# Input also laid out transposed; first chunk in four steps of input piece, weight piece and products; sum of squares from the pieces; identity products first

## Chip, core and metric

The kernel runs on one core of a Trainium2 chip. The metric is the time of one execution on the device in microseconds (us), as the median of several runs. Five engines work side by side and meet at semaphores: TensorE (PE: products and transposes into PSUM), VectorE (DVE), ScalarE (ACT), GpSimd (POOL) and SyncE (SP), which here only issues DMA transfers. An engine works through its own instructions in a fixed order.

## What is computed

Two macaron layers over 256 tokens of 1024 channels. The part in question is the start of the first feed-forward block (FFN):

```python
def rms_norm(x, gain):
    x32 = x.astype(jnp.float32)
    y = x32 * lax.rsqrt(jnp.mean(x32 * x32, axis=-1, keepdims=True) + EPS)
    return (y * gain.astype(jnp.float32)).astype(x.dtype)

def swiglu_ffn(x, w_in, w_out):
    gate, up = jnp.split(x @ w_in, 2, axis=-1)
    return (jax.nn.silu(gate) * up) @ w_out
...
for layer in range(DEPTH):
    g = norm_gains[layer]
    h = swiglu_ffn(rms_norm(x, g[0]), ffn_w_in[layer, 0], ffn_w_out[layer, 0])
    x = x + 0.5 * rms_norm(h, g[1])
    ...
```

After it come a causal convolution module or a gated linear recurrence, and a second FFN, in each layer.

## The kernel before

Tokens lie in two tiles of 128 (`xs[0]`, `xs[1]`, index t). An FFN has 11 chunks of 256 hidden channels. For each chunk, SP brings four weight pieces of 128x1024 fp32 for the way up (`w1`) and two for the way down (`w2`), each 512 KB, from one long array (`weight`, L115). A landed piece lies in one of 4 buffers `raw`; ACT rounds it to fp32r (`wh`) and DVE takes the rest (`wl = raw - wh`, `split`, L130 to L132). A piece's transfer waits until DVE has read the piece four before it. Every product is three PE products, hi by hi, hi by lo and lo by hi (`mm3`, L134 to L137).

The input needs to stand with channels on partitions. `pre_norm` (L160) does that: PE transposes 128x128 blocks through PSUM (L168), ACT multiplies by the gain and rounds (L172, into `xth`), DVE takes the rest (L178, into `xtl`). The factor 1/rms of a token is not needed for the products: `mean_square` (L151) sums the squares on ACT with an accumulator (L156), POOL adds and takes the power -0.5 (L146, L148, L158), and the factor goes into the sigmoid's scale and the products' finish (`up`, L316 to L320). Chunk 0 has the tokens on PSUM partitions (`project_both`, L222: 48 products of 512 columns, half for each token tile). All later chunks (`channels`, L274) have hidden channels there, 48 products of 256 columns for each half b of a chunk (L281 to L283), and need the token factors as a row tile, which `token_scales` (L262, L268) makes with two fp32 products.

At the start SP issues the first half of tile 0 of the input (256 KB), the gains, the second half, tile 1 (512 KB) and then the weight pieces in the order of the array: w1 of chunk 0, w2 of chunk 0, w1 of chunk 1, and so on. The Tile scheduler sets the order of each engine's instructions; `tc.issue_after` holds an instruction back behind another. The body calls `ffn(0, 0, first_weights, constants)`; `constants(c)` is called after chunk c and makes tables for later stages. `xs` is read again in `post_norm` (L200), at the end of the FFN.

Of the kernel before, what the change touches and what calls it, by code (L numbers as in the profile page):

```python
# [8 lines left out]
F32 = mybir.dt.float32  # L9
# [7 lines left out]
P = 128  # L17
D = 1024
# [22 lines left out]
def trunk_kernel(  # L41
    ctx: ExitStack,
    tc: tile.TileContext,
    x_in: bass.AP,
    wts: bass.AP,
    cols: bass.AP,
    rows: bass.AP,
# [20 lines left out]
    def b4(dtype=F32):  # L68
        return new(sb, [P, 1024], dtype, "b4", 10)
# [34 lines left out]
    nc.sync.dma_start(xs[0][:, :512], x_in[0, :P, :512])  # L104
    nc.sync.dma_start(gcol, cols)
    nc.sync.dma_start(xs[0][:, 512:], x_in[0, :P, 512:])
    nc.sync.dma_start(xs[1], x_in[0, P:, :])

    stream = [0]
    ahead = []  # L110
    last_hi = [None]
    last_split = [None]
    last_raw = [None]

    def weight(fine=False):  # L115
        n, half = divmod(stream[0], 2)
        stream[0] += 1
        src = new(sb, [P, 1024], F32, "raw", 4)
        last_raw[0] = nc.sync.dma_start(src, wts[n, :, half * 1024 : half * 1024 + 1024]).ins
# [3 lines left out]
        with ExitStack() as held:  # L123
            if stream[0] <= 4:
                held.enter_context(tc.issue_after(last_hi[0]))
            for a in range(0, 1024, step):
                split(hi[:, a : a + step], lo[:, a : a + step], src[:, a : a + step])
        return hi, lo

    def split(dst_h, dst_l, src):  # L130
        last_split[0] = act.copy(dst_h, src).ins  # L131
# [19 lines left out]
    def mean_square(src):  # L151
        junk = b4()
        ss = tiny(2)
        for n in range(2):
            sl = slice(n * 512, (n + 1) * 512)
            act.activation(junk[:, sl], src[:, sl], AF.Square, accum_out=ss[:, n : n + 1])  # L156
        tot = tiny()
        pool.tensor_tensor(tot, ss[:, 0:1], ss[:, 1:2], op=ALU.add)  # L158
        return rsqrt(tot, 1.0 / D, EPS)

    def pre_norm(t, gi):
        src = xs[t]
        hi, lo = xth[:, t * D : (t + 1) * D], xtl[:, t * D : (t + 1) * D]
        for h in range(2):
            pt = tr()
            for j in range(4):
                k = h * 4 + j
                pe.transpose(pt[:, j * P : (j + 1) * P], src[:, k * P : (k + 1) * P], ident)  # L168
            for j in range(4):
                k = h * 4 + j  # L170
                g = gcol[:, gi * KD + k : gi * KD + k + 1]
                last_hi[0] = act.activation(hi[:, k * P : (k + 1) * P],  # L172
                                            pt[:, j * P : (j + 1) * P], AF.Copy, scale=g).ins
# [8 lines left out]
        if gi == 0:  # L182
            return hi, lo, None
        return hi, lo, mean_square(src)

    def transposed(src, hi, lo, n, base, gain=None):
        pt = tr()
# [10 lines left out]
    def post_norm(t, accs, gain, share, bias=None):  # L198
# [17 lines left out]
        for n in range(2):  # L216
# [5 lines left out]
    def project_both(xt, ws):  # L222
        o = [mm(), mm()]
        for t, i in ((0, 0), (0, 1), (1, 0), (1, 1), (0, 2), (0, 3), (1, 2), (1, 3)):
            hi, lo, _ = xt[t]
            wh, wl = ws[i]
            for k in (2 * i, 2 * i + 1):
                sl = slice((k % 2) * 512, (k % 2) * 512 + 512)
                kp = slice(k * P, (k + 1) * P)
                mm3(o[t], hi[:, kp], lo[:, kp], wh[:, sl], wl[:, sl], k == 0, k == KD - 1)  # L230
        return o

    def project(t, xt, ws):
        o = mm()
# [55 lines left out]
    def start(gi, before):  # L290
        first = pre_norm(0, gi)
        before()
        second = pre_norm(1, gi)
        if gi == 0:
            with tc.issue_after(last_split[0]):
                return [(*first[:2], mean_square(xs[0])), (*second[:2], mean_square(xs[1]))]
        return [first, second]

    def ffn(layer, which, before, extra=None):
        base = layer * 3 + (0 if which == 0 else 2)  # L300
        xt = start(base, before)
        accs = [None, None]
        w1, w2, hid, raw, both = {}, {}, {}, {}, {}

        def fetch(c):
            if c not in w1:
                fine = c == 0 or extra is not None and c == 1
                w1[c] = ahead.pop() if ahead else [weight(fine) for _ in range(4)]
                w2[c] = [weight(fine) for _ in range(2)]

        def up(t, c, o):
            if o is None:
                o = project(t, xt[t], w1[c])
            r = xt[t][2]
            sig = narrow("e")
            act.activation(sig, o[:, :CH], AF.Sigmoid, scale=r)  # L316
            g = narrow("e")
            dve.scalar_tensor_tensor(g, o[:, :CH], r, sig, op0=ALU.mult, op1=ALU.mult)
            h = narrow("e")
            dve.scalar_tensor_tensor(h, o[:, CH:], r, g, op0=ALU.mult, op1=ALU.mult)  # L320
            raw[t, c] = h

        def turn(t, c):
            hi, lo = narrow("hid", F32R), narrow("hid", F32R)
            transposed(raw.pop((t, c)), hi, lo, 2, 0)
            hid[t, c] = blocks(hi, lo, 2)

        def up_both(c, b):
            fetch(c)
            if b == 0:  # L330
                both[c] = b4(F32R)
            gu = channels(w1[c], (b * P, CH + b * P), scales)
            h = narrow("e")
            act.activation(h, gu[:, :SEQ], AF.Sigmoid)  # L334
            dve.tensor_tensor(h, h, gu[:, :SEQ], op=ALU.mult)  # L335
            dve.tensor_tensor(h, h, gu[:, SEQ:], op=ALU.mult)  # L336
            hi = both[c][:, b * SEQ : (b + 1) * SEQ]
            lo = both[c][:, 512 + b * SEQ : 512 + (b + 1) * SEQ]
            split(hi, lo, h)
            for t in range(NT):  # L340
                ts_ = slice(t * P, (t + 1) * P)
                hid.setdefault((t, c), []).append((hi[:, ts_], lo[:, ts_]))

        def down(t, c):
# [370 lines left out]

    made = {}

    def first_weights():
        ahead.append([weight(True) for _ in range(4)])

    def constants(c):
        if c == 2:
            made["steps"] = tap_spectrum()
        if c == 4:
            made["steps"].pop(0)()
        if 5 <= c < 9:
            made["steps"].pop(0)()
        if c == 9:
            with tc.issue_after(last_split[0]), tc.issue_after(last_raw[0]):
                made["lower"] = lower_bound()  # L730

    def store(t):
# [4 lines left out]
    rest = ffn(0, 0, first_weights, constants)  # L737
    rest = conv_mixer(0, made["spectrum"], rest)
    rest = ffn(0, 1, rest)
    rest = ffn(1, 0, rest)  # L740
# [102 lines left out]
```

## Time and profile before

| | |
|---|---|
| median of 3 runs | 1032.33 us (1032.0 to 1032.75) |
| the profiled execution's own time | 1030.74 us |
| its span, first to last instruction | 1029.0 us |
| PE busy | 1004.7 us (98%) |
| DVE, ACT, POOL busy | 705.6, 504.7, 71.0 us |
| mean granted clock of PE | 0.996 |
| DMA | 181.14 MB, mean 176 GB/s |

The profile is of one execution. Its span is 1.74 us shorter than the time of the same execution. Shares of busy time are a mean over stages; for this change the first 42 us count. A row of the timeline gives the start, the length from the first start to the last end, the engine, line and operation, and in brackets the idle time of the engine ahead of it with what ended it. PE's products overlap one another, so that the distance from start to start, and not the length, is what one of them costs in a row of them.

### The profile page before, as it was taken

Reading aid. Unit: us, or ns where it says so; the run is one execution under the profiler, and the core shown is the slowest. Engines: PE = TensorE matmul, PEld = TensorE weight load, DVE = VectorE, ACT = ScalarE, POOL = GpSimd, SP = SyncE. Lnnn points to the kernel's source line nnn. Section 1 sums busy time; section 2 is a strip of 40 time slices with the busy share of each in tenths; the row PEclk is TensorE's granted clock in tenths of the full one; section 3 lists DMA queues with packets and bytes.
Section 4 is the critical chain, followed back from the end, with each engine's and each line's share of the span. In section 5 each row is a group of like instructions: output and inputs, shape, how many; then the busy total and the mean of one; then the engine's idle time right before and its main releaser. Section 6 shows DMA issues by size and latency. Waiting matters only on the chain. (4 is left out here: it accounts for less than half of the span.)

```text
span 1029.0 us, 16850 instructions
## 1 busy us (share of the span) xinstructions
PE 1004.7 (98%) x6676; PEld 913.2 (89%) x6676; DVE 705.6 (69%) x1092; ACT 504.7 (49%) x852; POOL 71.0 (7%) x116
## 2 busy tenths in 40 slices
PE   7999999999899999999999999999999999999997
PEld 6999999888779999998899999989888879999996
DVE  6766666899887565658675656677676586666663
ACT  7544444764485444446544444574143473444441
POOL 1000000000010000000100000021343020000000
PEclk9999999999999999999999999999999999999999
DMA  7756464843536465647464646555222555564641
GB/s 254 259 198 212 156 211 142 270 164 111 182 101 226 168 199 170 223 152 241 144 206 163 205 164 226 185 202 179 87 84 91 176 175 186 161 215 155 215 143 41
DMA packets 50510, 181.14 MB, mean 176 GB/s; under 512 B 5985, under 2 KB 6113, under 8 KB 50432
## 3 DMA queue, kind: packets, MB, share of 16 engines
q1 hardware_dynamic: 50432, 180.07, 52.6%
q8 instruction: 52, 0.85, 0.3%
q14 instruction: 26, 0.21, 0.1%
HBM read 179.00 MB, written 1.05 MB: 175 GB/s over the span
## 5 line engine op out<-in xcount | busy, mean ns | idle before, releaser
L132 DVE TENSOR_TENSOR wl<-raw,wh 128x1024 fp32r<-128x1024 f32 (+1 forms) x386 | 400.6, 1059 | 200.4 <-ACT wh L131 196.8
L131 ACT CAST wh<-raw 128x1024 fp32r<-128x1024 f32 (+1 forms) x386 | 336.5, 923 | 275.4 <-PE mm L282 127.5
L281 PE MATMUL mm<-xth,wh 128*128 128x256 f32 x1408 | 396.3, 281 | 0.0
L282 PE MATMUL mm<-xtl,wh 128*128 128x256 f32 x1408 | 396.3, 281 | 0.0
L283 PE MATMUL mm<-xth,wl 128*128 128x256 f32 x1408 | 396.0, 281 | 0.0
L281 PEld LDWEIGHTS mm<-xth,wh 128*128 128x128 f32 x1408 | 265.8, 189 | 3.2 <-DVE e L335 0.7
L282 PEld LDWEIGHTS mm<-xtl,wh 128*128 128x128 f32 x1408 | 265.1, 188 | 2.6
L283 PEld LDWEIGHTS mm<-xth,wl 128*128 128x128 f32 x1408 | 266.1, 189 | 0.5 <-DVE wl L132 0.2
L136 PE MATMUL acc<-wl,b 128*128 128x512 f32 x352 | 137.8, 391 | 0.0
L137 PE MATMUL acc<-wh,b 128*128 128x512 f32 x352 | 137.7, 391 | 0.0
L135 PE MATMUL acc<-wh,b 128*128 128x512 f32 x352 | 137.6, 391 | 0.0
L137 PEld LDWEIGHTS acc<-wh,b 128*128 128x128 f32 x352 | 66.1, 188 | 14.1
L135 PEld LDWEIGHTS acc<-wh,b 128*128 128x128 f32 x352 | 66.1, 188 | 11.5
L136 PEld LDWEIGHTS acc<-wl,b 128*128 128x128 f32 x352 | 66.1, 188 | 11.4
L334 ACT ACTIVATE e<-ga 128x256 f32<-128x256 f32 x80 | 33.4, 418 | 79.8 <-DVE ga L286 79.8
L242 PE MATMUL mm<-wh,xth 128*128 128x512 f32 x176 | 70.7, 401 | 0.0
L243 PE MATMUL mm<-wl,xth 128*128 128x512 f32 x176 | 70.1, 398 | 0.0
L286 DVE TENSOR_TENSOR ga<-mm,scales 128x512 f32<-128x512 f32 x88 | 60.2, 685 | 12.4 <-PE mm L283 12.2
L146 POOL TENSOR_SCALAR tiny<-tiny 128x1 f32<-128x1 f32 (+1 forms) x30 | 8.4, 281 | 802.6 <-ACT b L212 711.5
L131 ACT CAST b<-e 128x256 fp32r<-128x256 f32 x80 | 32.4, 405 | 53.2 <-DVE e L336 53.2
L246 PE MATMUL mm<-wh,xtl 128*128 128x512 f32 x176 | 49.8, 397 | 0.0
L132 DVE TENSOR_TENSOR b<-e,b 128x256 fp32r<-128x256 f32 x80 | 33.8, 422 | 21.3 <-ACT b L131 21.3
(156 smaller groups left out, 877.4 us busy)
## 6 DMA issues: line engine op xcount, KB each, us to landing
raw<-wts SPq DMA_DIRECT2D x328, 512.0 KB, 5.0
b<-rows SPq DMA_DIRECT2D x10, 512.0 KB, 6.1
out_dram<-x SPq DMA_DIRECT2D x4, 256.0 KB, 2.1
x<-x_in SPq DMA_DIRECT2D x2, 256.0 KB, 2.8
x<-x_in SPq DMA_DIRECT2D x1, 512.0 KB, 4.2
b<-dft SPq DMA_DIRECT2D x1, 371.0 KB, 4.6
ca<-masks SPq DMA_DIRECT2D x1, 192.0 KB, 4.8
b<-w_dw SPq DMA_DIRECT2D x1, 124.0 KB
```

Of the source, the lines that this page charges most:

```text
L131: last_split[0] = act.copy(dst_h, src).ins
L132: dve.tensor_tensor(dst_l, src, dst_h.bitcast(F32), op=ALU.subtract)
L135: pe.matmul(o, lh, rh, start=first, stop=False)
L136: pe.matmul(o, lh, rl, start=False, stop=False)
L137: pe.matmul(o, ll, rh, start=False, stop=last)
L242: pe.matmul(o, hi[:, kp], wh[:, sl], start=k == 0, stop=False)
L243: pe.matmul(o, hi[:, kp], wl[:, sl], start=False, stop=False)
L246: pe.matmul(o, a, w, start=False, stop=h == 1 and n == 3)
L281: pe.matmul(og, wh[:, cs], xkh[:, k], start=k == 0, stop=False)
L282: pe.matmul(og, wh[:, cs], xkl[:, k], start=False, stop=False)
L283: pe.matmul(og, wl[:, cs], xkh[:, k], start=False, stop=k == KD - 1)
L286: dve.tensor_tensor(pair(res), pair(o), scales.unsqueeze(1).broadcast_to([P, 2, SEQ]), op=ALU.mult)
```

## The change

The host also lays the input out transposed, as `x_turned`: four pieces of 128 partitions by two channel blocks by 256 tokens (256 KB each). A new function `boot` makes chunk 0:

- 22 fp32 products of the 128x128 identity with itself, into a PSUM tile that nothing reads, stand first on PE.
- Then four steps follow, kept in this order on ACT, DVE, PE and SP by `behind`. Step i takes input piece i (ACT rounds its two blocks, DVE takes the rests, from SBUF and for both token tiles at once), weight piece i, the six products of token tile 0 and the six of token tile 1. There are no transposes by PE in it.
- The squares of each piece are made by ACT in SBUF without an accumulator, and added by DVE to a running sum. In step 3, between the products of the two token tiles, PE multiplies that sum by a column of ones (4 products of 128x1), DVE finishes the mean and POOL takes the power, for both token tiles in one instruction.
- The accumulators of chunk 0 come from the pool `acc`, not `mm`.
- w1 of chunk 1 is fetched before w2 of chunk 0, and all pieces of chunks 0 and 1 are split in halves of 512 columns (as before).
- The gains are loaded by a DMA that ACT issues. `xs` is loaded from `x_in` (two DMAs of 512 KB) after chunk 3.

```diff
+        warm = tr()
+        for j in range(22):
+            sl = slice(j % 4 * P, (j % 4 + 1) * P)
+            pe.matmul(warm[:, sl], ident, ident, start=True, stop=True)
+
+        def turned(i):
+            src = part(pieces, i)
+            nc.sync.dma_start(src, x_turned[i])
+            for j in range(2):
...
+                act.activation(xkh[:, k], xk, AF.Copy, scale=g)
+                dve.scalar_tensor_tensor(xkl[:, k], xk, g, xkh[:, k].bitcast(F32),
+                                         op0=ALU.mult, op1=ALU.subtract)
...
+        for i in range(4):
+            with behind(act, dve, pe, nc.sync):
+                turned(i)
+            with behind(act, dve, pe, nc.sync):
+                ws.append(weight(True))
+                multiply(0, i)
+            with behind(act, dve, pe):
+                act.activation(part(squares, i), part(pieces, i), AF.Square)
+                if i > 0:
+                    dve.tensor_tensor(total, total, part(squares, i), op=ALU.add)
+            if i == 3:
+                with behind(dve, pe):
+                    for t in range(NT):
+                        for j in range(2):
+                            pe.matmul(pt[:, t : t + 1], total[:, (2 * j + t) * P : (2 * j + t + 1) * P],
+                                      ones[:, :1], start=j == 0, stop=j == 1)
+                    dve.tensor_scalar(ms, pt[:, :NT], 1.0 / D, EPS, op0=ALU.mult, op1=ALU.add)
+                    pool.tensor_tensor(r, ms, mhalf[:, :NT], op=ALU.pow)
+            with behind(pe):
+                multiply(1, i)
...
-        fetch(0)
-        o = project_both(xt, w1[0]) if extra is not None else [None, None]
-        up(0, 0, o[0])
-        up(1, 0, o[1])
+        if before is None:
+            stream[0] = 12
+            w1[1] = []
+            for n in range(4):
+                with behind(act, dve, nc.sync):
+                    w1[1].append(weight(True, 6 + n))
+                with behind(act, dve):
+                    if n < NT:
+                        up(n, 0, o[n])
+            with behind(act, dve, nc.sync):
+                w2[0] = [weight(True, 4 + n) for n in range(2)]
+            w2[1] = [weight(True, 10 + n) for n in range(2)]
...
     def constants(c):
+        if c == 3:
+            with behind(nc.sync):
+                for t in range(NT):
+                    nc.sync.dma_start(xs[t], x_in[0, t * P : (t + 1) * P, :])
```

What the scheduler makes of it, on PE at the program's start. Before (`tr` is a PSUM tile for transposes, `x_75` and `x_76` are the two token tiles, `mm_204` and `mm_205` their accumulators):

```order
L168 MATMUL tr_84<-ident,x_75 128x128 x4
L168 MATMUL tr_97<-ident,x_75 128x128 x4
L168 MATMUL tr_142<-ident,x_76 128x128 x4
L135 MATMUL mm_204<-wh_112,xth 128x512
L168 MATMUL tr_155<-ident,x_76 128x128 x4
L136 MATMUL mm_204<-wl_113,xth 128x512
```

and now, in the same place (`acc_85` and `acc_86` are the accumulators of the two token tiles):

```order
L198 MATMUL tr_90<-ident 128x128 x22
L136 MATMUL acc_85<-wh_120,xth 128x512
L137 MATMUL acc_85<-wl_121,xth 128x512
L138 MATMUL acc_85<-wh_120,xtl 128x512
L136 MATMUL acc_85<-wh_120,xth 128x512
L137 MATMUL acc_85<-wl_121,xth 128x512
L138 MATMUL acc_85<-wh_120,xtl 128x512
```

The transposes are gone, the identity products stand ahead, and the weight piece's products follow at once. On DVE, where chunk 0 goes over into chunk 1, before (`wl_191` and `wl_199` are w2 of chunk 0, `wl_284` the first piece of w1 of chunk 1, `e` the steps of the gated unit):

```order
L132 TENSOR_TENSOR wl_191<-raw_188,wh_190 128x512 x2
L132 TENSOR_TENSOR wl_199<-raw_196,wh_198 128x512 x2
L318 SCALAR_TENSOR_TENSOR e_256<-mm_204,tiny_176,e_254 128x256
L132 TENSOR_TENSOR wl_284<-raw_281,wh_283 128x512
L320 SCALAR_TENSOR_TENSOR e_258<-mm_204,tiny_176,e_256 128x256
L132 TENSOR_TENSOR wl_284<-raw_281,wh_283 128x512
```

and now, with the instructions' waits in brackets (`wl_201` is the last piece of w1 of chunk 0, `b_4_83` the sum of squares, `tr_87` its product with ones, `wl_229` and `wl_243` are the first two pieces of w1 of chunk 1):

```order
L133 TENSOR_TENSOR wl_201<-raw_198,wh_200 128x512 [waits Activation_49]
L228 TENSOR_TENSOR b_4_83<-b_4_83,b_5_84 128x512 [waits DVE_49,Activation_49]
L235 TENSOR_SCALAR tiny_88<-tr_87 128x2 [waits PE_49]
L133 TENSOR_TENSOR wl_229<-raw_226,wh_228 128x512 [waits DMAHW1_49,Activation_49]
L133 TENSOR_TENSOR wl_229<-raw_226,wh_228 128x512 [waits Activation_49]
L364 SCALAR_TENSOR_TENSOR e_236<-acc_85,tiny_89,e_234 128x256 [waits Activation_49]
L366 SCALAR_TENSOR_TENSOR e_238<-acc_85,tiny_89,e_236 128x256 [waits DVE_49]
L133 TENSOR_TENSOR wl_243<-raw_240,wh_242 128x512 [waits DMAHW2_49,Activation_49]
```

The rests of chunk 1's weights now stand behind an instruction (L235) that waits for PE, and w2 of chunk 0 has gone behind w1 of chunk 1. From the first products of chunk 2 on, PE has the same instructions in the same order in both kernels.

## Rows read from the trace of the kernel before

**Rows 1.** The page: busy time, share and number of instructions of each engine, and PE's busy tenths in 40 slices of the span.

```profile
PE 1004.7 (98%) x6676; PEld 913.2 (89%) x6676; DVE 705.6 (69%) x1092; ACT 504.7 (49%) x852; POOL 71.0 (7%) x116
PE   7999999999899999999999999999999999999997
```

**Rows 2.** Busy time of each engine in stretches of the first 35 us: us, then PE, its weight loads, DVE, ACT and POOL with their number of instructions, the granted clock, the DMA engines' share and GB/s.

```profile
0.00:5.00 5.00, 1.31 (x5) 0.94 (x6) 0.00 (x0) 1.98 (x4) 0.88 (x8) 1.00 0.59 179
5.00:10.00 5.00, 2.49 (x9) 1.63 (x9) 2.75 (x9) 2.93 (x9) 0.00 (x0) 1.00 0.98 350
...
25.00:30.00 5.00, 5.00 (x35) 4.42 (x34) 5.00 (x10) 3.32 (x8) 0.26 (x1) 1.00 0.73 206
30.00:35.00 5.00, 5.00 (x41) 4.83 (x40) 2.56 (x5) 1.96 (x3) 0.00 (x0) 1.00 0.86 301
```

**Rows 3.** Timeline of PE at the start.

```profile
3.38 1.09 PE L168 MATMUL tr<-ident,x 128*128 128x128 f32 x4 [3.38 <-DMA x<-x_in]
4.78 1.12 PE L168 MATMUL tr<-ident,x 128*128 128x128 f32 x4 [0.31 <-DMA x<-x_in]
6.87 1.12 PE L168 MATMUL tr<-ident,x 128*128 128x128 f32 x4 [0.97 <-DVE xtl L178]
9.52 0.80 PE L135 MATMUL mm<-wh,xth 128*128 128x512 f32 x1 [1.54 <-ACT wh L131]
...
11.82 0.63 PE L135 MATMUL mm<-wh,xth 128*128 128x512 f32 x1
12.25 0.63 PE L136 MATMUL mm<-wl,xth 128*128 128x512 f32 x1
...
14.38 0.46 PE L135 MATMUL mm<-wh,xth 128*128 128x512 f32 x1
14.68 0.39 PE L136 MATMUL mm<-wl,xth 128*128 128x512 f32 x1
14.91 0.40 PE L137 MATMUL mm<-wh,xtl 128*128 128x512 f32 x1
```

**Rows 4.** Timeline of PE where chunk 0's products end and chunk 1's begin, and at the first product of chunk 2.

```profile
23.31 0.40 PE L137 MATMUL mm<-wh,xtl 128*128 128x512 f32 x1
23.55 0.38 PE L189 MATMUL tr<-ident,e 128*128 128x128 f32 x2
...
24.12 0.28 PE L281 MATMUL mm<-xth,wh 128*128 128x256 f32 x1
24.24 0.28 PE L282 MATMUL mm<-xtl,wh 128*128 128x256 f32 x1
...
25.18 0.63 PE L268 MATMUL tr<-e,ones 128*128 128x128 f32 x4
25.67 0.41 PE L189 MATMUL tr<-ident,e 128*128 128x128 f32 x2
...
41.62 0.28 PE L281 MATMUL mm<-xth,wh 128*128 128x256 f32 x1
```

**Rows 5.** PE's groups of instructions by line and form, with the number, the busy time and the mean length of one in ns: transposes at the start (stretch 9 to 24 us) and later (23 to 42 us).

```profile
L168 PE MATMUL tr<-ident,x 128*128 128x128 f32 x4 | 1.1, 420 | 0.0
...
L189 PE MATMUL tr<-ident,e 128*128 128x128 f32 x4 | 0.8, 279 | 0.0
```

**Rows 6.** The clock in a later stretch, where PE had been idle, in the columns of rows 2.

```profile
266.00:268.00 2.00, 1.25 (x8) 0.88 (x7) 2.00 (x5) 1.78 (x6) 0.00 (x0) 0.77 0.02 8
268.00:270.00 2.00, 2.00 (x11) 2.00 (x11) 2.00 (x6) 1.91 (x7) 0.00 (x0) 0.50 0.76 248
270.00:272.00 2.00, 2.00 (x12) 1.82 (x12) 1.35 (x4) 2.00 (x6) 0.00 (x0) 0.87 0.62 203
```

**Rows 7.** Timeline of PE in that stretch, the last instruction ahead of which it was idle.

```profile
267.77 1.12 PE L454 MATMUL tr<-ident,b 128*128 128x128 f32 x4 [0.72 <-ACT b L461]
```

**Rows 8.** Timeline of POOL: the identity made at the start, and the power for one token tile.

```profile
1.15 0.29 POOL masks.py:199 TENSOR_SCALAR_AFFINE_SELECT ident<-ident 128x128 f32<-128x128 f32 x1
...
17.78 1.00 POOL L148 TENSOR_TENSOR tiny<-tiny,mhalf 128x1 f32<-128x1 f32 x1
```

**Rows 9.** Timeline of ACT from the first weight piece to chunk 1.

```profile
8.85 1.14 ACT L131 CAST wh<-raw 128x512 fp32r<-128x512 f32 x2 [1.77 <-DMA raw<-wts]
10.15 1.14 ACT L131 CAST wh<-raw 128x512 fp32r<-128x512 f32 x2 [0.16 <-DMA raw<-wts]
11.44 2.40 ACT L131 CAST wh<-raw 128x512 fp32r<-128x512 f32 x4 [0.15 <-DMA raw<-wts]
...
16.37 0.67 ACT L156 ACTIVATE b<-x 128x512 f32<-128x512 f32 x1
16.89 0.24 ACT L156 ACTIVATION_READ_ACCUMULATOR b<-x 128x1 f32 x1
...
21.01 0.48 ACT L316 ACTIVATE e<-mm,tiny 128x256 f32<-128x256 f32 x1 [0.58 <-PE mm L137]
21.38 2.17 ACT L131 CAST wh<-raw 128x512 fp32r<-128x512 f32 x4
```

**Rows 10.** Timeline of DVE: the rests of chunk 0's weights, a step of the gated unit, and rests of the weights that chunk 1 works with.

```profile
9.50 5.14 DVE L132 TENSOR_TENSOR wl<-raw,wh 128x512 fp32r<-128x512 f32 x8 [1.27 <-ACT wh L131]
...
21.52 0.48 DVE L318 SCALAR_TENSOR_TENSOR e<-mm,tiny,e 128x256 f32<-128x256 f32 x1 [0.20 <-ACT e L316]
...
25.44 4.89 DVE L132 TENSOR_TENSOR wl<-raw,wh 128x512 fp32r<-128x512 f32 x8
```

**Rows 11.** Around the place to which the load of `xs` goes: timeline of ACT, the first cast of chunk 4's weights and a later group of four, and of PE, the first product of chunk 4.

```profile
62.11 1.05 ACT L131 CAST wh<-raw 128x1024 fp32r<-128x1024 f32 x1 [3.87 <-DMA raw<-wts]
...
70.62 3.90 ACT L131 CAST wh<-raw 128x1024 fp32r<-128x1024 f32 x4 [2.33 <-PE mm L282]
...
75.38 0.28 PE L281 MATMUL mm<-xth,wh 128*128 128x256 f32 x1
```

More of the change, by code (lines that the diff above doesn't have):

```diff
@@ L44, in trunk_kernel @@
     x_in: bass.AP,
+    x_turned: bass.AP,
     wts: bass.AP,
@@ L103, in trunk_kernel, with behind, weight @@
     gcol = const.tile([P, G_END], F32, name="gcol")
[L104 to L107, printed above, removed]
+    act.dma_start(gcol, cols)
     stream = [0]
[L110 to L117, printed above, removed]
+    def behind(*engines):
+        held = ExitStack()
+        for eng in engines:
+            last = next((i for i in reversed(nc.cur_bb.bb.instructions) if i.engine == eng.engine), None)
+            if last is not None:
+                held.enter_context(tc.issue_after(last))
+        return held
+    def weight(fine=False, at=None):
+        if at is None:
+            at = stream[0]
+            stream[0] += 1
+        n, half = divmod(at, 2)
         src = new(sb, [P, 1024], F32, "raw", 4)
-        last_raw[0] = nc.sync.dma_start(src, wts[n, :, half * 1024 : half * 1024 + 1024]).ins
+        nc.sync.dma_start(src, wts[n, :, half * 1024 : half * 1024 + 1024])
         hi = new(sb, [P, 1024], F32R, "wh", 10)
@@ L122, in weight @@
         step = 512 if fine else 1024
[L123 to L127, printed above, removed]
+        for a in range(0, 1024, step):
+            split(hi[:, a : a + step], lo[:, a : a + step], src[:, a : a + step])
         return hi, lo
     def split(dst_h, dst_l, src):
-        last_split[0] = act.copy(dst_h, src).ins
+        act.copy(dst_h, src)
         dve.tensor_tensor(dst_l, src, dst_h.bitcast(F32), op=ALU.subtract)
@@ L171, in pre_norm @@
                 g = gcol[:, gi * KD + k : gi * KD + k + 1]
-                last_hi[0] = act.activation(hi[:, k * P : (k + 1) * P],
-                                            pt[:, j * P : (j + 1) * P], AF.Copy, scale=g).ins
+                act.activation(hi[:, k * P : (k + 1) * P],
+                               pt[:, j * P : (j + 1) * P], AF.Copy, scale=g)
             for j in range(4):
@@ L181, in pre_norm, with boot, multiply @@
                 )
-        if gi == 0:
-            return hi, lo, None
         return hi, lo, mean_square(src)
+    def boot():
+        pieces = [b4(), b4()]
+        squares = [b4(), b4()]
+        ws, o = [], [acc(), acc()]
+        pair = lambda ap: ap.rearrange("p (t m) -> p t m", m=P)
+        part = lambda bufs, i: bufs[i // 2][:, i % 2 * 512 : (i % 2 + 1) * 512]
+        total = squares[0][:, :512]
+        pt = tr()
+        ms, r = tiny(NT), tiny(NT)
+        warm = tr()
[6 more added lines that the diff above has]
+            for j in range(2):
+                k = 2 * i + j
+                g = gcol[:, k : k + 1]
+                xk = pair(src[:, j * SEQ : (j + 1) * SEQ])
+                act.activation(xkh[:, k], xk, AF.Copy, scale=g)
+                dve.scalar_tensor_tensor(xkl[:, k], xk, g, xkh[:, k].bitcast(F32),
+                                         op0=ALU.mult, op1=ALU.subtract)
+        def multiply(t, i):
+            wh, wl = ws[i]
+            hi, lo = xth[:, t * D : (t + 1) * D], xtl[:, t * D : (t + 1) * D]
+            for k in (2 * i, 2 * i + 1):
+                sl = slice((k % 2) * 512, (k % 2) * 512 + 512)
+                kp = slice(k * P, (k + 1) * P)
+                mm3(o[t], hi[:, kp], lo[:, kp], wh[:, sl], wl[:, sl], k == 0, k == KD - 1)
+        for i in range(4):
[18 more added lines that the diff above has]
+                multiply(1, i)
+        xt = [(xth[:, t * D : (t + 1) * D], xtl[:, t * D : (t + 1) * D], r[:, t : t + 1])
+              for t in range(NT)]
+        return xt, ws, o
@@ L220, in post_norm @@
             )
[L222 to L231, printed above, removed]
     def project(t, xt, ws):
@@ L293, in start @@
         second = pre_norm(1, gi)
-        if gi == 0:
-            with tc.issue_after(last_split[0]):
-                return [(*first[:2], mean_square(xs[0])), (*second[:2], mean_square(xs[1]))]
         return [first, second]
@@ L300, in ffn @@
         base = layer * 3 + (0 if which == 0 else 2)
-        xt = start(base, before)
         accs = [None, None]
         w1, w2, hid, raw, both = {}, {}, {}, {}, {}
+        if before is None:
+            xt, w1[0], o = boot()
+        else:
+            xt = start(base, before)
         def fetch(c):
             if c not in w1:
-                fine = c == 0 or extra is not None and c == 1
-                w1[c] = ahead.pop() if ahead else [weight(fine) for _ in range(4)]
+                fine = c == 0
+                w1[c] = [weight(fine) for _ in range(4)]
                 w2[c] = [weight(fine) for _ in range(2)]
@@ L347, in down @@
             expand(accs[t], hid.pop((t, c)), w2[c], c == 0, c == NC - 1)
-        fetch(0)
-        o = project_both(xt, w1[0]) if extra is not None else [None, None]
-        up(0, 0, o[0])
-        up(1, 0, o[1])
+        if before is None:
+            stream[0] = 12
[9 more added lines that the diff above has]
+            w2[1] = [weight(True, 10 + n) for n in range(2)]
+        else:
+            fetch(0)
+            for t in range(NT):
+                up(t, 0, None)
         turn(0, 0)
@@ L716, in trunk_kernel @@
     made = {}
-    def first_weights():
-        ahead.append([weight(True) for _ in range(4)])
     def constants(c):
+        if c == 3:
+            with behind(nc.sync):
+                for t in range(NT):
+                    nc.sync.dma_start(xs[t], x_in[0, t * P : (t + 1) * P, :])
         if c == 2:
@@ L728, in constants @@
         if c == 9:
-            with tc.issue_after(last_split[0]), tc.issue_after(last_raw[0]):
+            with behind(act, nc.sync):
                 made["lower"] = lower_bound()
@@ L735, in store @@
             nc.sync.dma_start(out[0, t * P : (t + 1) * P, sl], xs[t][:, sl])
-    rest = ffn(0, 0, first_weights, constants)
+    rest = ffn(0, 0, None, constants)
     rest = conv_mixer(0, made["spectrum"], rest)
@@ L821 @@
         "x_in": i["x"],
+        "x_turned": i["x"][0].T.reshape(4, 2, P, SEQ).transpose(0, 2, 1, 3).reshape(4, P, 2 * SEQ),
         "wts": _layout(np, i),
```

## The prediction

> **What bounds the kernel now.** I read the page's busy times first: PE works for 1004.7 of 1029.0 us, and the only one of 40 slices with a low digit at the beginning is the first [rows 1]. The change touches nothing behind it, so the table by stretches comes next: in the first 5 us PE is busy 1.31 us and in the next 2.49 us, then it is full, while DVE is full from 25 to 30 us and half idle from 30 to 35 us [rows 2]. PE's own timeline says what the first 10 us consist of: 3.38 us until the first input piece, 0.31 and 0.97 us between groups of transposes, 1.54 us until the first weights are rounded; together 6.2 us of idle time [rows 3]. It says a second thing: the first products start 0.43 us apart (11.82, 12.25), from 14.68 us on 0.23 us apart [rows 3]. [...] The 38 products from 14.68 to 23.55 us take 8.87 us, 0.233 us each [rows 3, 4].
>
> From 23.55 us (end of chunk 0's products) to 41.62 us (first product of chunk 2) there are 18.07 us, and PE is not idle in them [rows 2, 4]. From 41.62 us on both kernels have the same PE order, so whatever is gained by then is carried to the end, as long as weights are ready ahead of need. The forecast is therefore the new time of that one product.
>
> **Identity products.** They need the identity, which POOL finishes at 1.15 + 0.29 = 1.44 us [rows 8]; PE starts at about 1.5 us. How long is one? The two fp32 products of `token_scales` show as four passes, so a product is two [rows 4]. A pass, from start to start: at the lower clock four transposes in 1.12 us, of which the last is 0.42 long, so (1.12 - 0.42)/3 = 0.23; at the upper clock (0.38 - 0.28)/1 = 0.10, and 25.18 to 25.67 gives 0.12 [rows 3 to 5]. I take 0.22 and 0.11: a product costs 0.44 and 0.22 us, all 22 of them 9.7 or 4.8 us.
>
> When does the clock rise? Before, it rose at about 14.4 us, 4.9 us after the first product of a stretch without idle time, behind transposes with gaps [rows 3]. Elsewhere the level fell and came back: shares of 0.77, 0.50 and 0.87 over three times 2 us put the lower level between about 267.1 and 270.5 us, so it rose 2.7 us after PE was last idle at 267.77 us [rows 6, 7]. Those are the two ends, 2.7 and 4.9 us. I take 4.9, since it is the row of the same state, a start from idle: a rise at 6.4 us. Then 4.9/0.44 = 11.1 products are done, the other 10.9 take 2.4 us, and PE is free at **8.8 us**. With 2.7 us it would be 7.7 us; with no rise at all 11.2 us.
>
> [...]
>
> **Are the data there by 8.8 us?** The first input piece lands as before, at about 3.3 us (first in SP's queue, 256 KB). The first weight piece has 256 KB ahead of it; before, the first 512 KB of input and the gains had landed at 4.78 us and 1 MB of input by 6.87 us at the latest [rows 3], so its 768 KB land between. Two casts and rests behind it (0.62 + 0.69 us to the first) end by 8.2 us. The fourth weight piece has the same 3 MB up to its end as before, 11.44 + 1.30 = 12.7 us [rows 9]. PE needs 12 x 0.233 = 2.8 us a step and comes to step 3 at 17.2 us. Per step ACT has two blocks (0.37 each, from 21.01 to 21.38), two casts ((2.17 - 0.62)/3 = 0.52 each) and the squares (0.52): 2.3 us [rows 9]. DVE has two rests of the input (0.4 to 0.48 each), two of the weights and, in three steps, the sum (each (4.89 - 0.69)/7 = 0.60): 2.6 to 2.8 us [rows 10]. Started at about 6.7 us, four DVE steps end at 17.1 to 17.9 us; PE wants the last rest at 18.1 us. So chunk 0 is PE's, with DVE close behind it.
>
> **Chunk 0.** 48 products x 0.233 = 11.2 us. The small sums add four fp32 products of one column; no row shows such a one. Their weight loads are as wide as those of `token_scales`, whose four passes take 0.49 us [rows 4]; eight passes cost at most 1.0 us and at least nothing. I take 0.9, near the upper end. End of chunk 0: 8.8 + 11.2 + 0.9 = **20.9 us**, against 23.55 before: 2.65 us. Removed with it: 16 transposes and 16 narrow operations each on ACT and DVE, and the four reads of the accumulator (0.24 each [rows 9]), all of them in the stretch that is replaced as a whole.
>
> **The new wait.** DVE's L235 waits for PE's small sums; behind it are queued the rests of chunk 1's weights. PE ends the sums at 8.8 + 42 x 0.233 + 0.9 = 19.5 us; DVE finishes the mean at 19.7 and the rest of chunk 1's first piece (two of 0.60) at 20.9 us, when PE wants it. POOL's power takes 1.00 us [rows 8], so the token factor is there at about 20.8 us, ACT's sigmoid runs for 0.37 us, and only behind it stands the cast of chunk 1's second piece, ready at 21.9 us. PE gets there after six products of 0.12 us [rows 4], at 21.6 us, and waits 0.3. With the wait for the gated unit's result just behind, I put **0.4 us** here (0 to 1.0). After that DVE has eight rests and four steps of the unit in 4.8 + 1.7 us, ends at 26.5 to 27 us, and PE comes to the last of them at about 27.1 us. Chunk 2 starts at 20.9 + 18.07 + 0.4 = 39.37 us: **2.25 us earlier**.
>
> **What costs nothing, and its cover.** The load of `xs` puts 1 MB more on SP's queue, ahead of chunk 4's weights. At 1.30 us for 512 KB [rows 9] that is 2.6 us. The first of these weights is cast at 62.11 us, on landing, and needed at 75.38; the four from 70.62 us wait for PE and not for data [rows 11]. 13 us of cover; without it the 2.6 us would be the whole gain. `xs` itself is read at the end of the FFN. The gains' DMA moves from SP to ACT, where it delays the table load; ACT has nothing to do before 3.3 us. Nothing else on POOL or SP moves past work that is waited for.
>
> **Sum.** Span 1029.0 - 2.25 = 1026.75 us, own time 1030.74 - 2.25 = 1028.5 us; the shown median is 1.59 us above that execution, and from it the same subtraction gives 1032.33 - 2.25 = 1030.1 us.
>
> **Rivals.** (1) *The identity products don't lift the clock* (slower). If PE's clock responds to the real products only, the 22 end at 11.2 us and the products run at 0.43 us until 4.9 us later: 11.4 of them, then 36.6 x 0.233 = 8.5 us, plus 0.9: chunk 0 ends at 25.5 us, 1.95 us later than now; with the 0.4 us that is +2.35 us, 1034.7 us. It decides from a rise later than about 11 us on (at 11.2 us the end would be 23.3). Against it: they are as dense as the transposes and products behind which it rose at 270.5 us [rows 6, 7]. For it: the transposes of the first 8 us did not lift it, though those had gaps [rows 3]. 0.10. (2) *DVE becomes the bound* (no change). It is full from 25 to 30 us already [rows 2], gets three sums more and a wait in front of chunk 1. If its operations are a sixth longer than the rows say, four steps take 12.9 us instead of 11 and end at 19.6, 1.5 us after PE wants them, and the twelve behind cost another 0.8 us: nothing is left, 1032.3 us. For it: its margin is only some tenths. Against it: the same operation has the same length in all rows. 0.17. (3) *The clock rises early*, 2.7 us after the first identity product, and the small sums cost half: 1.1 + 0.45 more, -3.8 us, 1028.5 us. 0.08.
>
> **How the numbers follow.** The forecast has 0.65. Its own ends: a rise 2 us later than taken (-1.0), a wait of 1.0 (-0.6), against a rise at 2.7 (+1.1) and small sums for nothing (+0.9): gains of 0.65 to 4.2 us, mostly 1.2 to 3.4. About 0.2% (2.06 us) is what a measurement of this kernel can tell from no change; the forecast lies just beyond it, so I give 0.43 of its 0.65 to faster and 0.22 to the same. Faster 0.43 + 0.08 = 0.51, same 0.22 + 0.17 = 0.39, slower 0.10. The range reaches from the early rise (1028.4) to the second rival (1032.5); the first is left out.
>
> **What would show it.** PE's timeline: identity products from 1.5 us, their distance falling from 0.44 to 0.22 us at about 6.4 us, products from 8.8 us 0.23 us apart without idle time, the small sums at about 18.6 us, and the first product of chunk 2 at 39.4 us; PE's list of waits without the 3.4, 1.5 and 1.0 us of the input, the weights and the transposes. If products start 0.43 us apart, it is the first rival. If PE shows waits for `wl` in the steps or in chunk 1, it is the second. Wrong altogether would be a chunk 2 at 39.4 us and a kernel no faster: then a later stage had slack that took the gain.

## The result, and the profile after

| | before | after |
|---|---|---|
| median | 1032.32 us (1032.0 to 1033.04, 6 runs) | 1038.23 us (1035.38 to 1040.04, 6 runs) |
| profiled execution's span | 1029.0 us | 1038.2 us |
| PE, DVE, ACT busy | 1004.7, 705.6, 504.7 us | 1012.4, 706.4, 503.1 us |

The ratio is 1.0054, 95% interval 1.004 to 1.0069: slower by about 6 us, and outside the range of the prediction. The profile is of the longest of the six executions (1040.04 us), so that it shows more lost than the median does. On the page of the changed kernel PE is busier by 7.7 us [rows 1], and the granted clock, in tenths for 40 slices, is below full in the third slice (52 to 78 us) and the eleventh:

```profile
PE 1012.4 (98%) x6712; PEld 920.4 (89%) x6712; DVE 706.4 (68%) x1088; ACT 503.1 (48%) x840; POOL 69.6 (7%) x111
...
PEclk9989999999899999999999999999999999999999
```

The start first: the timeline of PE in the changed kernel, against [rows 3] and [rows 4].

```profile
1.49 7.93 PE L198 MATMUL tr<-ident 128*128 128x128 f32 x44 [1.49 <-POOL ident masks.py:199]
9.18 0.48 PE L136 MATMUL acc<-wh,xth 128*128 128x512 f32 x1
9.49 0.40 PE L137 MATMUL acc<-wl,xth 128*128 128x512 f32 x1
9.73 0.39 PE L138 MATMUL acc<-wh,xtl 128*128 128x512 f32 x1
...
19.05 0.95 PE L233 MATMUL tr<-ones,b 128*128 128x1 f32 x8
19.86 0.47 PE L136 MATMUL acc<-wh,xth 128*128 128x512 f32 x1
...
21.34 0.28 PE L327 MATMUL mm<-xth,wh 128*128 128x256 f32 x1
...
22.46 0.38 PE L327 MATMUL mm<-xth,wh 128*128 128x256 f32 x1 [0.25 <-ACT wh L132]
...
39.90 0.28 PE L327 MATMUL mm<-xth,wh 128*128 128x256 f32 x1
```

The start does what it was to do. Products start 0.23 us apart from 9.73 us on, the distance of the upper clock in [rows 3], no piece of input or weights is waited for in chunk 0, and chunk 2 begins at 39.90 us, 1.72 us earlier than the 41.62 us of [rows 4]. The loss lies behind it. PE's list of waits (what waited, total us, times, longest) has a new first entry, and PE's timeline has its place:

```profile
PE acc L136 <- ACT b L132: 5.0, 1, 5.0
```

```profile
64.33 0.39 PE L138 MATMUL acc<-wh,b 128*128 128x512 f32 x1
69.69 0.80 PE L136 MATMUL acc<-wh,b 128*128 128x512 f32 x1 [4.98 <-ACT b L132]
70.29 0.63 PE L137 MATMUL acc<-wl,b 128*128 128x512 f32 x1
...
82.51 0.28 PE L327 MATMUL mm<-xth,wh 128*128 128x256 f32 x1
```

The last row is the first product of chunk 4, which stood at 75.38 us [rows 11]: 7.13 us later now, after chunk 2 had begun 1.72 us earlier. In the middle PE waits 4.98 us for `b`, the rounded hidden units of chunk 2's second half. The table by stretches (columns as in rows 2) shows what comes with it:

```profile
64.00:66.00 2.00, 0.72 (x4) 0.25 (x2) 0.00 (x0) 0.00 (x0) 0.00 (x0) 1.00 0.14 57
66.00:68.00 2.00, 0.00 (x0) 0.00 (x0) 0.00 (x0) 0.00 (x0) 0.00 (x0) 1.00 0.07 27
68.00:70.00 2.00, 0.31 (x1) 0.31 (x2) 0.63 (x1) 1.71 (x3) 0.00 (x0) 0.68 0.07 27
70.00:72.00 2.00, 1.94 (x4) 1.03 (x4) 2.00 (x4) 0.62 (x1) 0.00 (x0) 0.50 0.24 55
72.00:74.00 2.00, 2.00 (x9) 1.80 (x8) 1.48 (x4) 0.42 (x1) 0.00 (x0) 0.50 0.79 270
74.00:76.00 2.00, 2.00 (x13) 2.00 (x13) 0.46 (x2) 0.40 (x1) 0.00 (x0) 0.61 0.57 209
```

From about 64.7 to 68.3 us no engine works, and from 66 to 68 us the DMA engines move 27 GB/s at a share of 0.07: 0.07 x 16 = 1.1, an estimate of about one engine's time of 16. By the shares of 0.68 and 0.61 the clock is at its lower level, granted 0.50, from about 68.7 us, still in the wait, to about 75.5 us. The products at 71.58, 72.00 and 72.43 us stand 0.42 to 0.43 us apart there, those from 63.18 to 64.33 us, at 1.00, 0.23: the two distances of [rows 3]. The shares missing from 1.00 in the last three rows (0.50, 0.50, 0.39, over 2 us each) are an estimated 2.8 us of work not done. The sum of 8.85 us from 1.72 ahead to 7.13 behind is then 4.98 (wait) + 2.8 (clock) and about 1 us of small losses, of which PE's timeline shows one at 42.91 us (0.47 us, for a rest on DVE). Who keeps PE waiting is to be seen on ACT and on SP:

```profile
57.01 0.42 ACT L380 ACTIVATE e<-ga 128x256 f32<-128x256 f32 x1
68.29 1.04 ACT L132 CAST wh<-raw 128x1024 fp32r<-128x1024 f32 x1 [10.86 <-DMA raw<-wts]
69.24 0.40 ACT L132 CAST b<-e 128x256 fp32r<-128x256 f32 x1
```

```profile
50.97 0.42 SPq L747 DMA_DIRECT2D b<-dft  x1
51.44 0.33 SPq L749 DMA_DIRECT2D b<-w_dw  x1
51.81 0.87 SPq L780 DMA_DIRECT2D x<-x_in  x2
55.27 4.70 SPq L123 DMA_DIRECT2D raw<-wts  x4
```

`b` is cast by an instruction that stands, in ACT's fixed order, behind the cast of chunk 4's first weights, and that cast waited 10.86 us for its data (3.87 us in [rows 11]). Ahead of these weights SP had issued two tables, `dft` and the 31 rows of `w_dw` (the taps of the convolution, 4 KB a row), and then the reload of `xs`. The time from issue to landing of the four weight pieces behind them, least, median and most, is in the kernel before and in the changed one:

```profile
DMA to landing us min/median/max: 5.4/5.8/6.1
```

```profile
DMA to landing us min/median/max: 12.4/12.8/13.1
```

Later, the clock falls once more where it fell before [rows 6], here for twice as long (0.88, 0.50, 0.50, 0.50 and 0.91 in steps of 2 us from 272 to 282 us). The span of this execution ends 9.2 us later than before.

### The profile page after: what moved, and what is told of

Read it like the earlier page. It is cut to its first block, busy times and chain, and to the rows that moved or that the text cites. A ratio compares the mean times of both kernels' runs of the same rounds, so it can differ in the third digit from the quotient of the medians.

```text
span 1038.2 us, 16911 instructions
## 1 busy us (share of the span) xinstructions
PE 1012.4 (98%) x6712; PEld 920.4 (89%) x6712; DVE 706.4 (68%) x1088; ACT 503.1 (48%) x840; POOL 69.6 (7%) x111
## 6 DMA issues: line engine op xcount, KB each, us to landing
x<-x_in SPq DMA_DIRECT2D x2, 512.0 KB, 14.3
```

## Experiments

All are compared with the kernel before, run beside them on the same chip: its medians are 1032.73 us (first four kernels), 1032.82 (next four) and 1032.87 (last three).

The theory was a chain: the reload stands behind a table that one DMA engine carries (the author's estimate, from the share of 0.07), the weights behind both land late, ACT's order puts the cast of `b` behind them, PE waits and the clock falls. One rival: the start itself is the loss, by its identity products or its new order of weights. Another: late weights cost by themselves, whatever ACT's order. The first five kernels took the links apart.

The reload moved to the end of chunk 6, away from the tables:

```diff
-        if c == 3:
+        if c == 6:
             with behind(nc.sync):
```

> The changed kernel with the load of the input tiles moved from chunk 3 to chunk 6; nothing else. Theory A (the load stands in the queue right behind the 31-row table of taps, which one DMA engine carries alone; chunk 4's weights land 6 us later, and the cast of a chunk's own hidden units stands behind their cast on ACT): PE's 5.0 us wait for the cast of b and the lower clock from 68.7 us are gone, first product of chunk 4 at about 73.1 us instead of 82.5, time 1029.3 to 1031 us. Theory B (the earlier start itself makes chunk 4's weights late, since DMA has not become earlier by 50 us): a wait of 2 us or more stays at the same place, 1033 us or more. Theory C (the 1 MB has to be paid wherever it stands): a wait of some 2.6 us or more appears around chunk 6 or 7, 1033 us or more.

Measured: 1032.19 us (1030.19 to 1035.03), ratio 0.9998 (0.9987 to 1.0009). The reload at its place was worth 6 us. The time is above theory A's range and below that of the others: what this left open is why it isn't lower than before.

The table padded to 32 rows, the reload left at chunk 3:

```diff
-        nc.sync.dma_start(taps[:W_CONV], w_dw)
+        nc.sync.dma_start(taps[: W_CONV + 1], w_dw)
...
-        "w_dw": i["conv_w_dw"][0],
+        "w_dw": np.pad(i["conv_w_dw"][0], ((0, 1), (0, 0))),
```

> [...] Theory A (it is the one DMA engine with 31 rows of 4 KB): the pieces behind land within 1 us of one another on all engines, the wait falls from 5.0 us to under 1 us, time 1029.5 to 1031.5 us. Theory C (it is the 1 MB of the reload): chunk 4's weights still land 2.6 us or more later than before, the wait is 2 us or more, time 1034 us or more.

Measured: 1031.79 us, ratio 0.9987 (0.9977 to 0.9997). That is 0.3 us above theory A's range. 4 KB more to move take 6 us away; the two pieces of `x_in` land after 9.1 us (median) instead of 14.3.

The kernel before, with a reload of `xs` put behind the table, as the change does it, and nothing else of the change:

```diff
-        nc.sync.dma_start(taps[:W_CONV], w_dw)
+        made["taps"] = nc.sync.dma_start(taps[:W_CONV], w_dw).ins
...
+            for t in range(NT):
+                with tc.issue_after(made["taps"]):
+                    made["taps"] = nc.sync.dma_start(xs[t], x_in[0, t * P : (t + 1) * P, :]).ins
```

> The kernel before with the two input tiles loaded once more, right behind the table of taps, as in the changed kernel (the values are the same). Theory A: the cast of chunk 4's first weights and that of b behind it move from 62.1 and 63.1 to about 68 and 69 us; PE wants b at about 67 us in this kernel and waits some 2.7 us; with or without a stretch at the lower clock behind it 1035 to 1037.5 us. Theory B: the reload is hidden here, 1032.3 us.

Measured: 1037.99 us, ratio 1.0057 (1.0043 to 1.0072), the whole loss without the new start, and 0.5 us more than expected. In its profile the two pieces of the reload land after 12.6 us (median) and PE waits 2.3 us for `b`. The first rival falls.

The kernel with the reload at chunk 6, without identity products:

```diff
-        warm = tr()
-        for j in range(22):
-            sl = slice(j % 4 * P, (j % 4 + 1) * P)
-            pe.matmul(warm[:, sl], ident, ident, start=True, stop=True)
```

> As e1_reload_at_6, without the 22 identity products. If they pay by lifting the clock early: products start at about 7.3 us 0.43 us apart, the clock rises some 4.9 us later or more, chunk 0 ends at 21.7 us or later instead of 21.3, and the time is 0.3 to 2 us above that of e1. If they only hold the products up: chunk 0 ends at 19 to 20 us and the time is 1 us or more below e1.

Measured: 1032.65 us, ratio 1.0003 (0.999 to 1.0016), the same as with them. In its profile PE waits 6.61 us for the first weights and begins with products 0.43 us apart, yet chunk 2 begins at 39.80 us (39.93 with 22). It also shows the stall again, without a reload near: 2.09 us for `b` at 66.34 us, with products 0.43 us apart behind it.

The link on ACT alone. Reload and table stay as the change has them; only the casts change places, one instruction on ACT and one on DVE:

```diff
...
+                with ExitStack() as held:
+                    if c == 4 and before is None:
+                        for ins in first_cast:
+                            held.enter_context(tc.issue_after(ins))
-                w1[c] = [weight(fine) for _ in range(4)]
+                    w1[c] = [weight(fine) for _ in range(4)]
...
```

(`first_cast` holds the cast and the rest of chunk 2's second half.)

> The changed kernel with one instruction moved on ScalarE and one on VectorE: the cast of chunk 2's second half of hidden units stands ahead of the cast of chunk 4's first weights instead of behind it. The reload of the input stays where the change put it, behind the table of 31 rows, so the weights land as late as before. Theory (the reload costs through the order on ScalarE): the wait of 5.0 us for the hidden units is gone, the clock does not fall at 68 us, chunk 4 begins near 74 us instead of 82.5, and the time is 1031 to 1033 us. Rival (late transfers themselves are the price, since the weights of chunk 4 come too late for their own products): a wait for the weights takes its place at chunk 4, and the time stays above 1035 us.

Measured: 1031.74 us, ratio 0.9984 (0.9975 to 0.9992). ACT in this kernel:

```profile
59.26 0.41 ACT L390 CAST b<-e 128x256 fp32r<-128x256 f32 x1 [1.96 <-DVE e L387]
67.32 1.05 ACT L132 CAST wh<-raw 128x1024 fp32r<-128x1024 f32 x1 [7.65 <-DMA raw<-wts]
```

The weights are as late as in the changed kernel (12.7 us to landing), ACT waits about as long (1.96 and 7.65 us), and PE doesn't wait for `b`: chunk 4 begins at 73.64 us. The second rival falls, though not to nothing: in the products of chunk 4, from 75.6 to 82.5 us, PE loses 1.1 us of its lead, which the late transfers can account for. The place of one small cast behind them cost most of the 6 us.

The next three asked where the start's gain of 1.7 us had gone in the kernels with the reload at chunk 6. The theory was a wall: a stretch at 195 to 210 us with full DMA engines (shares of 0.89, 1.02 and 0.53 in steps of 5 us in the kernel before), which would take any lead away.

```diff
-        for j in range(22):
+        for j in range(12):
```

> The kernel with the reload at chunk 6 and 12 identity products instead of 22; they end near 6.8 us, about when the first weights are cast (6.6 us), where those of 22 end at 9.2 us. Theory (with 22 the identity products themselves hold back the first products, and without any the clock's late rise costs as much): the first product starts at 6.8 us, the clock rises near 7.3 us, and chunk 1 begins up to 2.1 us earlier than 21.4 us, less what the pieces after the first make it wait. Rival (the pieces of input and weights set the pace): the products wait for the third and fourth piece and chunk 1 still begins after 20.8 us. Of whatever is won, the theory of the wall at 195 to 210 us (the DMA engines are full there and weights land at the same time by the clock on the wall, however early the chunk began) leaves little: the time is 1031 to 1032.5 us, within 0.7 us of the kernel with 22; if there is no wall, it is 1030 to 1030.8.

Measured: 1031.04 us, ratio 0.9986 (0.9976 to 0.9996). In its profile chunk 1 begins at 19.61 us, 1.73 us ahead of the changed kernel, and the lead is gone by 69 us: PE's waits at the hidden units are back, with weight pieces that land after 9.0 us, and the lower clock behind them (granted 0.50 from 66 to 68 us).

```profile
63.67 0.50 PE L136 MATMUL acc<-wh,b 128*128 128x512 f32 x1 [1.12 <-ACT b L132]
64.96 0.50 PE L138 MATMUL acc<-wh,b 128*128 128x512 f32 x1 [0.56 <-DVE b L133]
```

So the table of 31 rows alone is enough for the stall, if PE comes early.

The same with 32:

```diff
-        for j in range(22):
+        for j in range(32):
```

> The kernel with the reload at chunk 6 and 32 identity products instead of 22: the first product starts 2.2 us later (11.4 us instead of 9.2) and chunk 2 begins 2.2 us later (42.1 us instead of 39.9, which is 0.5 us later than before the change). With a wall at 195 to 210 us, the lead that is lost was worth little behind it: products behind 216 us are later by 0.6 to 1.2 us than with 22 identity products, and the time is 1032.5 to 1033.5 us. Without a wall all 2.2 us are lost: 1034 to 1035 us.

Measured: 1036.51 us (1031.95 to 1039.81), ratio 1.0027 (1.0011 to 1.0043); above what either theory expected. Chunk 2 begins at 42.15 us as expected, but the profiled execution has the stall (1.6 us for `b`) and, at the products behind it, is later than the kernel before by 4.7 us. And the wall is none: from 201 to 216 us this kernel and the one with 12 fall back another 0.5 and 0.8 us against the kernel before, though they come there later than it, with no lead to take.

All three edits together, as in the diffs above: reload at chunk 6, 32 rows, 12 identity products.

> The reload at chunk 6, the table of taps padded to 32 rows (the row added holds zeros and is not used), and 12 identity products. If the three add up without meeting a wall, 1029.5 to 1030.5 us; if the stretch of full DMA engines at 195 to 210 us takes what the start wins, 1031 to 1032 us, like the kernels with one of the three alone.

Measured: 1029.33 us (1028.94 to 1029.56), ratio 0.9966 (0.9953 to 0.9979), the fastest of all. Nothing is lost at 66 us. The last three kernels split this up. The same with 22 identity products, which is the change with a reload that is out of the way:

> All three edits, but with the 22 identity products of the change: what the change is worth once its reload costs nothing. By the prediction's sum, chunk 2 begins 2.25 us earlier than before; by the trace of the changed kernel 1.7 us. With 1.7 us and nothing lost behind it: 1029.8 to 1030.8 us, 0.5 to 1 us above the kernel with 12. If the reload's delay is not all that the change lost, above 1031.5 us.

Measured: 1030.27 us, ratio 0.9977 (0.9967 to 0.9987). The same without identity products:

> All three edits, without any identity product. Theory (the identity products win nothing at 22, because the first products could start at 6.6 us and run at half clock while the identity products of the 22 still run): chunk 2 begins within 0.3 us of where it does with 22, and the time is within 0.5 us of it. Rival (they are worth the 2.35 us that the prediction gave them): 2 us above the kernel with 22.

Measured: 1029.66 us, ratio 0.9965 (0.9952 to 0.9979). Its PE starts like this:

```profile
6.80 0.79 PE L136 MATMUL acc<-wh,xth 128*128 128x512 f32 x1 [6.80 <-ACT wh L132]
7.53 0.80 PE L137 MATMUL acc<-wl,xth 128*128 128x512 f32 x1
...
9.40 0.63 PE L138 MATMUL acc<-wh,xtl 128*128 128x512 f32 x1
9.83 0.55 PE L136 MATMUL acc<-wh,xth 128*128 128x512 f32 x1
10.21 0.40 PE L137 MATMUL acc<-wl,xth 128*128 128x512 f32 x1
```

Chunk 2 begins at 38.87, 39.05 and 39.20 us with 12, 22 and 0 of them. And the kernel before with the table of 32 rows alone:

> The kernel before with the table of taps padded to 32 rows and nothing else. If the table costs the kernel before only now and then (the transfers behind it are late on one queue and the cast of chunk 2's hidden units has about 2 us to spare), its runs lie closer together and the median is 1031.3 to 1032.5 us; then the 3 us between the kernel before and the one with all three edits are mostly the start's. If the padded table alone brings those 3 us, it is below 1030.5 us.

Measured: 1033.24 us (1031.78 to 1034.48), ratio 1.0 (0.9992 to 1.0008). That is above the range expected: the padding gives the kernel before nothing, and its runs lie hardly closer together (1031.78 to 1034.48 us against 1031.54 to 1035.73). What the three edits gain is then the new start's.

## Why the prediction was wrong

**The step that failed** is "What costs nothing, and its cover". It priced the reload at 2.6 us and set against it 13 us of cover, from the first cast of chunk 4's weights (62.11 us) to their use (75.38 us) [rows 11]. Both halves were wrong.

- *The cover.* The cast's own user was looked up, but not the instruction queued behind the cast on ACT. In the kernel before, that is the cast of `b`, and PE wants `b` 10 us earlier than the weights (65.58 against 75.38 us):

```profile
62.11 1.05 ACT L131 CAST wh<-raw 128x1024 fp32r<-128x1024 f32 x1 [3.87 <-DMA raw<-wts]
63.06 0.40 ACT L131 CAST b<-e 128x256 fp32r<-128x256 f32 x1
```

```profile
65.35 0.39 PE L137 MATMUL acc<-wh,b 128*128 128x512 f32 x1
65.58 0.39 PE L135 MATMUL acc<-wh,b 128*128 128x512 f32 x1
```

  From 63.06 + 0.40 to 65.58 us there are 2.1 us of cover, not 13 (the row of 65.58 us is the seventh product of the twelve, the first that reads the second half). The 3.87 us in brackets in rows 11 said that ACT stood still for these data; that was the sign to ask who stood behind it. The kernel with the two casts exchanged shows that this is nearly the whole of it: with the weights as late it takes 1031.74 us, and 1030.27 us where they aren't late.
- *The price.* 1 MB at the pace of [rows 9] is 2.6 us, but the pieces behind it landed 7 us later (12.8 against 5.8 us). The trace shows the DMA engines at a share of 0.07 meanwhile. That one engine was behind, with the rows of the table, is the author's estimate from it, and the runs agree with that: with 22 identity products the weight pieces land after 7.1 us with 31 rows and 5.4 us with 32 if the reload is at chunk 6, and the two pieces of the reload after 14.3 and 9.1 us if it is at chunk 3. So does the count of packets, here with the reload at chunk 6, first with 31 rows and then with 32:

```profile
DMA packets 50942, 182.19 MB, mean 177 GB/s; under 512 B 6033, under 2 KB 6161, under 8 KB 50864
```

```profile
DMA packets 50958, 182.19 MB, mean 177 GB/s; under 512 B 6048, under 2 KB 6176, under 8 KB 50880
```

  Beside the added row there are 15 more packets under 512 B. In the changed kernel's trace a packet of 4 bytes stands behind each eight of 4 KB (at 66.49, 67.76 and 69.03 us); if one stands behind each engine's part of a transfer, 15 more fit sixteen parts in the place of one. And from 66.5 to 69.0 us the changed kernel's packets (number, MB, share of 16 engines) come one behind another, 0.16 us each, and fill the time of about one engine (6.1% x 16 = 0.98):

```profile
q1 hardware_dynamic: 16, 0.06, 6.1%
```

  If one engine carries all 31 rows, they are 31 packets of 0.16 us, an estimated 5 us by which it is behind; that the transfers behind the table land late by as much, because each has a part on that engine, is the author's estimate too. In the kernel before the same table cost no time (1033.24 us with 32 rows, 1032.87 beside it with 31): no reload followed there, SP issued the next piece only when a buffer came free, at 56.08 us, and the 2.1 us were left.
- *The clock.* The prediction put nothing on a fall of it. Behind the wait of 4.98 us it was granted 0.50 to about 75.5 us, which cost another 2.8 us by the estimate above.

**Identity products.** Start at 1.5 us: right. Clock: the starts of single passes in the trace are 0.213 us apart to 7.20 us and 0.11 us after it, as taken, but the rise came 5.7 us behind the start and not 4.9; PE was free at 9.18 and not 8.8 us. That differs between executions: in the five traces with the same 22 products PE was free at 8.34, 8.66, 8.70, 9.18 and 9.21 us, on either side of the 8.8. But their worth was misjudged. Rival 1 priced a start without their help at +2.35 us, because it left them standing in front. Without any, the first product begins at 6.6 to 6.8 us, since the first weights are cast by then, the products stand 0.43 us apart instead of 0.23 for 3 to 4.7 us, and that loses what the wait for the 22 costs. "Are the data there by 8.8 us?" was answered with yes; when they are there first was the better question.

**Chunk 0, small sums, new wait.** Chunk 0's end came at 21.34 us for 20.9, nearly all of it the later start; the small sums take 0.81 us (19.05 to 19.86) for 0.9; chunk 1 takes 18.56 us for 18.47, with the wait for the second piece's cast where it was expected (0.25 us at 22.46). Chunk 2 began 1.72 us earlier for 2.25 in this execution, 2.57 us earlier in that of the kernel with all edits and 22 identity products. In the five traces with 22 products it began at 39.05 to 39.93 us, around the 39.37 forecast. That step was right, and so was the sum: with the reload away and 32 rows, 0.9977 of the time before against the prediction's 0.9978. That these agree so closely is partly luck. The lead isn't simply carried to the end: in the one trace of that kernel 1.2 us of it are lost between 208 and 217 us and 1.2 us more near 266 us, where the clock falls in the trace before (3.4 us at 0.50, by the shares of [rows 6]); it ends 0.3 us behind that trace, whose own execution lies 1.6 us under its kernel's median.

**Rival 2** (DVE becomes the bound) didn't come about: no product of chunk 0 waits for a rest, and DVE is busy for 1.09 of the 5 us from 15 to 20 us:

```profile
10.00:15.00 5.00, 5.00 (x23) 4.04 (x22) 5.00 (x11) 4.84 (x11) 0.00 (x0) 1.00 1.00 385
15.00:20.00 5.00, 5.00 (x28) 4.18 (x27) 1.09 (x2) 1.02 (x2) 0.00 (x0) 1.00 0.51 161
```

**What would have made it wrong** was named ("a chunk 2 at 39.4 us and a kernel no faster"), with slack in a later stage as the cause. It was not slack but a new wait, and no rival had it: the slower one given 0.10 was of another kind.

**Open.** Of the four kernels with 31 rows and the reload at chunk 6, three profiles show the stall (0, 12 and 32 identity products); that with 22, of one of its fastest executions, doesn't. With 22, 0 and 12 products the mean granted clock is 0.993 or 0.994 in just the two or three slowest executions of each and 0.995 to 0.998 in the others, which fits a stall in some executions only. With 32 there is no such split (eight of twelve executions have 0.995 and take 1034.61 to 1038.74 us), so that its loss is explained for the profiled execution alone. From 208 to 217 us several profiled executions lose 0.4 to 1.3 us on the kernel before, while ACT waits for weights, others nothing; and the fall of the clock near 266 us lasts 3.4 us in some profiles (the kernel before, the reload at chunk 6) and 6.8 in others (the changed kernel, the one without identity products), by the shares missing from 1.00. Neither was followed to its cause. No record says which engine carried a packet: that one engine is behind rests on the padded table, the share of 0.07, the packets that come one behind another and the two counts.

## What to carry to other kernels

The cover of a delayed transfer isn't the time until its data are used. It is the time until anything is needed that stands behind the instruction that waits for it, on every engine whose order is fixed; a bracket on an engine that is not the bottleneck tells where to look. Here it was 2.1 us, and not 13. Before a transfer is put into a queue, see what is ahead of it there and how late what stands behind that lands: 7.1 us after issue behind this table of 31 rows, 5.4 us behind 32. Instructions that only raise the clock earned nothing here (1030.27 us with 22, 1029.33 with 12, 1029.66 with none), where the real ones could have run, slowly, in their time.

## What was not expected of the hardware

- A table of 124 KB in 31 rows delayed the 512 KB pieces behind it from 5.4 us (32 rows) to 7.1 us with 22 identity products, and the two pieces of a reload right behind it from 9.1 to 14.3 us; a 32nd row of zeros undid it.
- After a wait of 5.0 us PE's clock stayed at its lower level to about 75.5 us (granted 0.50 from 70 to 74 us, 0.61 from 74 to 76), although PE had no idle time from 69.69 us on; behind two waits of 1.1 and 0.6 us in the kernel with 12 identity products the clock fell as well (granted 0.50 from 66 to 68 us).
- From a start at rest, the passes of the 22 dense identity products went from 0.213 to 0.11 us apart 5.7 us after the first in the changed kernel's trace; by the times at which PE was free of them (8.34 to 9.21 us) it was an estimated 4.0 to 5.8 us in the five traces. Where none stood ahead, the real products went from 0.43 to 0.24 us apart 3 to 4.7 us after the first.
